# The front of a chunked SSD scan moved into the projection stage of a one-core decoder layer

## The chip, the core and the metric

The kernel runs on one core of one Trainium2 chip. The metric is the device time of one execution in microseconds. The core has TensorE (PE in the profile), VectorE (DVE), ScalarE (ACT), GpSimd (POOL) and SyncE (SP), which issues nearly all of the DMA transfers, in its own order. Each engine runs its instructions in order, and an instruction that waits holds up everything behind it on that engine.

## The reference

One layer of a hybrid decoder for 1024 prompt tokens and 8 samples of 8 new tokens, all in float32. The change touches the Mamba-2 (SSD) branch, which the reference computes in chunks of 128 tokens:

```python
def layer(x, ...):
    x = x + 0.5 * swiglu(rmsnorm(x, norm_ffn1), ffn1_w_in, ffn1_w_out)
    x = x + token_mixing(rmsnorm(x, norm_mix), ...)
    x = x + 0.5 * swiglu(rmsnorm(x, norm_ffn2), ffn2_w_in, ffn2_w_out)

# token_mixing
proj = hn @ w_in                          # u, z, xbc, dt, two gates
branch_pool = pool_mix(u_ext, ...) @ pool_w_out
xbc_c, new_conv = causal_conv(xbc, ...)   # depthwise, width 4, then SiLU
xs, bm, cm = split(xbc_c)                 # 32 heads of 64; 4 groups of B and C, 128 states
dt = softplus(dt_raw + dt_bias)
y, new_ssm = ssd_scan(xs, dt, A, bm, cm, h0)
yg = rms_per_group((y + d_skip * xs) * silu(z))
merged = gate0 * branch_pool + gate1 * ((yg * ssd_norm) @ ssd_w_out)
return merged @ w_o

# ssd_scan, per chunk of 128 tokens
a_cs = cumsum(dt * A);  xdt = x * dt
decay = exp(where(causal, a_cs[l] - a_cs[s], -inf))
cb = einsum('bclgn,bcsgn->bcgls', C, B)
y_diag = einsum('bcgrls,bcsgrp->bclgrp', cb[:, :, :, None] * decay, xdt)
st = einsum('bclgn,bclgr,bclgrp->bcgrpn', B, exp(a_cs[-1] - a_cs), xdt)
h = h * exp(a_cs[-1]) + st                # carried from chunk to chunk
y_off = einsum('bclgn,bcgrpn,bclgr->bclgrp', C, h_prev, exp(a_cs))
```

## The kernel before

The work goes through four stages: the first FFN, the projection (`in_proj`), the mixing stage (`mix`) and the second FFN. Activations lie turned, channels on the partitions and tokens along the row, in two halves `h`: 512 prompt tokens, then 512 prompt tokens and the 64 sample tokens (576). Float32 products are made of three fp32r products (high by high, high by low, low by high); `split` makes the high part on ACT and the low part on DVE, and `load_w` and `wino_weights` do the same with each piece of weight.

The order is written by hand with generators. Dense products run on PE and advance a clock `pe[0]` of nominal PE time; after each few products `tick()` takes every side chain that is due one step further, and a chain says with `yield` how much PE time it lets pass until its next step. `STEP`, `POST`, `RIPE`, `GP` and `MP` are such paces. `tc.high_priority` moves the splitting of weights and the emptying of accumulators ahead of other rows.

In the projection stage `proj_pair` computes two tiles of 128 channels for both halves at once; `done` hands each finished tile to `post_conv` (x, B and C), `post_u`, `post_z` or `post_gate`, whose generators stand in the list `work` and are run one after the other by `worker`. `post_conv` makes the convolution with three DVE instructions (L939), applies SiLU on ACT (L945) and writes the tile to DRAM (`convd`). Tiles of this stage come from a ring `fx` of 17 buffers, and small PSUM tiles from a ring `ps` of 2 banks.

In the mixing stage the dense work is the pool branch (`pgm`, `pbp`), the SSD output product (`pso`) and the output projection (`pwo`). Beside it one chain, `scan`, goes through 8 groups (two halves by four groups of heads), 4 chunks each and one chunk of samples (`smp`) in the second half. Per chunk `ssd_a` loads the cumulated decays spread over all partitions (`ab`), turns x on PE (`pxT`, L167), forms C B on PE and turns B on PE (both in `pcb`), masks C B on DVE (`cbm`, L1312), copies the turned B on ACT (`btok`, L1316), scales the turned x twice on DVE (`xdt`, L1318; `xd`, L1327), and makes the decays on ACT (`ea`, L1335; `ab`, L1337 and L1338) and multiplies them by the masked C B on DVE (L1339). `ssd_st` makes the chunk's state (`pst`, L163) and `ssd_b` the outputs (`pyo`, `pyd`). `gating` and `rstd` follow each group (`pss` sums squares on PE), then `ssd_out` and `merge` use the result. `fetch` loads a group's B, C (`bc`) and x (`xs`) one group ahead. The ring `act` of 42 buffers is shared by all stages; the mixing stage's own tiles lie where the projection's `fx` tiles were.

Of the kernel before, what the change touches and what calls it, by code (L numbers as in the profile page):

```python
# [43 lines left out]
STEP = (5.0, 3.8)  # L44
STEP_S = 1.0
POST, RIPE = 1.0, 3.0
GP = (1.5, 1.2)
# [14 lines left out]
def tile_hybrid_pool_ssd_macaron(  # L62
# [189 lines left out]
    acs_d = [dp.tile([4, NH, CH], F32, tag=f"acsd{h}", name=f"acsd{h}") for h in HALVES]  # L252
# [7 lines left out]
    convd, zd, gd, dhd, dld = (spill(*a) for a in (("cv", 24), ("zd", 16), ("gd", 16), ("dh", KD), ("dl", KD)))  # L260
    xnd = [dp.tile([P, NTOK[0]], F32, tag=f"xn{k}", name=f"xnd{k}") for k in range(KD)]
# [107 lines left out]
    def rstd(tiles, h, count, out, pace=1.0):  # L369
# [13 lines left out]
        yield 2.0 * max(pace, 0.75)  # L383
# [443 lines left out]
    def mix_dt(h, xs):  # L827
# [9 lines left out]
        def chain():  # L837
# [13 lines left out]
            e, s, q, dA = t1[:, 160 : 160 + n], t1[:, 320 : 320 + n], t2[:, :n], t2[:, 160 : 160 + n]  # L851
            dt, acs, dtd, cd = all_[:, :n], all_[:, 160 : 160 + n], all_[:, 320:448], all_[:, 448:576]
# [28 lines left out]
            dma(acs_d[h].rearrange("c h l -> (c h) l"), afm)  # L881
            V.tensor_tensor(dtd, dtd, dt[:, :128], op=ALU.mult)
# [19 lines left out]

    uhist = cp.tile([P, KD, HIST], F32, tag="uhist", name="uhist")
# [6 lines left out]
    def post(gen):  # L910
        work.append((pe[0] + RIPE, gen))
# [12 lines left out]
    def post_conv(h, ct, raw, new):  # L924
# [21 lines left out]
        dma(convd[h][ct], t[:, :N])  # L946
        yield POST / 2
# [112 lines left out]
    def proj_pair(kind, ia, ib, xs):  # L1060
# [4 lines left out]
        while len(work) > 4:  # L1065
            poster[0].step()
# [16 lines left out]
        def after(p, i, bk):  # L1083
# [3 lines left out]
            if p == "1":  # L1087
                out[i] = {"a": fx(name="ra"), "b": fx(name="rb")}
# [161 lines left out]
    def spread(Bf, xs4):  # L1250

        out = []
        for i in range(2):
            tok = slice(512 + 32 * i, 544 + 32 * i)
            xr = act((P, 5, 96), name="xr")
            S.copy(xr[:, :4, :].rearrange("p j (r t) -> p j r t", r=3), xs4[:, :, tok].unsqueeze(2).broadcast_to([P, 4, 3, 32]))
            S.copy(xr[:, 4, :].rearrange("p (r t) -> p r t", r=3), Bf[:, tok].unsqueeze(1).broadcast_to([P, 3, 32]))
            out.append(xr)
        return out
# [20 lines left out]
    def ssd_a(h, g, c, Bf, Cf, xs4, dts, h0s):  # L1280
# [11 lines left out]
        for q in range(nq):  # L1292
            ab = act((P, hq, L), name="ab")
            if smp:
                dma(ab, acs_sd[g * HPG : (g + 1) * HPG].partition_broadcast(P))
            else:
                r0 = g * HPG + q * hq
                dma(ab, acs_d[h][c, r0 : r0 + hq].partition_broadcast(P))
            abs_.append(ab)
        if smp:  # L1300
            xrs = spread(Bf, xs4)
            h0s.update({i: load_state(g, u) for i, u in enumerate(UNITS[:3])})
        yield
# [7 lines left out]
        cbm = small((P, P), "cbm", 2)  # L1311
        V.tensor_tensor(cbm[:L, :L], pb[:L, :L], tri_s if smp else tri, op=ALU.mult)  # L1312
        btok = None
        if not smp:
            btok = small((P, P), "btok", 2)
            S.copy(btok, pb[:, 128:256])  # L1316
        xp = act((P, 512), name="xdt")
        V.tensor_tensor(xp[:L, :].rearrange("p (h d) -> p h d", d=HD), px[:L, :].rearrange("p (h d) -> p h d", d=HD),  # L1318
                        dt[:L, hcs].unsqueeze(2).broadcast_to([L, HPG, HD]), op=ALU.mult)
        if smp:  # L1320
            xd = []
# [3 lines left out]
        else:  # L1325
            xd = act((P, 512), name="xd")
            V.tensor_tensor(xd[:L, :].rearrange("p (h d) -> p h d", d=HD), px[:L, :].rearrange("p (h d) -> p h d", d=HD),  # L1327
                            dtd[:L, hcs].unsqueeze(2).broadcast_to([L, HPG, HD]), op=ALU.mult)
        G.tensor_tensor(xs4[:, :, tok], xs4[:, :, tok], Dcol[:, g * 4 : g * 4 + 4].unsqueeze(2).broadcast_to([P, 4, L]), op=ALU.mult)
        ea = act((P, 4, L), name="ea")  # L1330
        for q, ab in enumerate(abs_):
            av = ab.rearrange("p (q h) l -> p q h l", h=2)
            ev = ea[:, q * (hq // 2) : (q + 1) * (hq // 2), :]
            for hh in range(2):
                S.activation(ev[hh * HD : (hh + 1) * HD], av[hh * HD : (hh + 1) * HD, :, hh, :], AF.Exp)  # L1335
            for i in range(hq):
                S.activation(ab[:L, i, :], ab[:L, i, :], AF.Relu, bias=acs[:L, hc + q * hq + i : hc + q * hq + i + 1], scale=-1.0)  # L1337
            S.activation(ab[:L], ab[:L], AF.Exp, scale=-1.0)  # L1338
            V.tensor_tensor(ab[:L], ab[:L], cbm[:L, :L].unsqueeze(1).broadcast_to([L, hq, L]), op=ALU.mult)  # L1339
# [10 lines left out]
    def ssd_b(h, g, c, a, hold, Cf, y4, dts, h0s):  # L1350
# [8 lines left out]
        if smp:  # L1359
# [12 lines left out]
            for i, (pr, bh) in enumerate(units):  # L1372
# [12 lines left out]
                dma(dst, h0)  # L1385
                if pr == 3:
# [19 lines left out]
        for i in range(HPG):  # L1406
            m_ = abs_[i // abs_[0].shape[1]][:L, i % abs_[0].shape[1], :]
# [32 lines left out]
    def ssd_group(h, g, Bf, Cf, xs4, dts, zs):  # L1440
# [3 lines left out]
        for c in range(4 + h):  # L1444
            ga = ssd_a(h, g, c, Bf, Cf, xs4, dts, h0s)
            next(ga)
            if c == 3:
# [310 lines left out]
```

## Time and profile before

| what | value |
| --- | --- |
| median of 3 runs | 2921.1 us (2917.12 to 2922.39) |
| the profiled execution | 2922.54 us |
| its span | 2920.7 us, 52612 instructions |
| mean granted TensorE clock | 0.99 |
| PE busy | 2829.0 us, 97% |
| DVE, ACT, POOL busy | 1715.2, 1374.7, 1001.9 us |
| HBM read, written | 361.77 MB, 143.05 MB |

Time is read on PE, which is busy 97% of the span: what counts is what fills it and where it stands still. The mixing stage runs from 1505 to 2166 us of the span, the projection from 803 to 1505 us.

### The profile page before, as it was taken

The page shows a single profiled execution, that of the slowest core. Times are in us where ns is not written, and L with a number is a line of the kernel's source. Part 1 is how long each engine was busy: PE and PEld are TensorE (multiplying, and loading weights), DVE is VectorE, ACT ScalarE, POOL GpSimd, SP SyncE. Part 2 cuts the span into 40 slices and gives each one's busy share as a digit, 9 for nine tenths or more (in the row PEclk, how much of TensorE's full clock was granted, in tenths as well). Part 3 has the DMA queues.
Part 4 walks back from the last instruction along what each step waited for, and adds up shares of the span by engine and source line. Part 5 has one row for each costly group of instructions (what it writes and reads, how often), then busy time and mean ns, then how long its engine had stood idle before and what let it go on. Part 6 is the DMA issues. An engine that isn't in the chain of part 4 may idle for free.

```text
span 2920.7 us, 52612 instructions
## 1 busy us (share of the span) xinstructions
PE 2829.0 (97%) x19306; PEld 2612.3 (89%) x19306; DVE 1715.2 (59%) x2722; ACT 1374.7 (47%) x3024; POOL 1001.9 (34%) x1088
## 2 busy tenths in 40 slices
PE   7999999999999999999989999889999999999998
PEld 6999999789989999999977887678999999997898
DVE  6555555434383586766767777866665544453432
ACT  5444444323354555554556665576233444442322
POOL 6444444000132355464712332322134444440000
PEclk9999999999999999999999999999999999999999
DMA  4575454856445554633377777785774522236642
GB/s 136 165 226 183 159 170 132 284 184 192 120 128 164 162 191 155 201 111 124 107 232 247 242 229 227 242 265 176 247 233 146 165 92 82 78 109 209 217 155 73
DMA packets 530340, 508.09 MB, mean 174 GB/s; under 512 B 36885, under 2 KB 374665, under 8 KB 530073
## 3 DMA queue, kind: packets, MB, share of 16 engines
q1 hardware_dynamic: 530064, 504.72, 54.6%
q8 instruction: 152, 2.49, 0.4%
q14 instruction: 108, 0.88, 0.1%
q10 hardware_dynamic: 16, 0.00, 0.0%
HBM read 361.77 MB, written 143.05 MB: 173 GB/s over the span
## 4 chain that ended last, share of the span: by engine, by line
PE 47%; DVE 4%; DMA 3%; ACT 2%; issue 1%; SPq 1%; POOL 0%; POOLq 0%; ACTq 0%; DVEq 0%
PE pw L163 24%; PE po L163 9%; PE pso L163 4%; PE pbp L163 3%; PE pwo L163 2%; PE pg L163 1%; PE pu L163 1%; ACT ab L1337 1%; PE pyd L163 1%; PE pst L163 1%; DVE ab L1339 1%; DMA ab<-acsd 0%; PE pyo L163 0%; DVE xs L1484 0%; DMA wh<-part 0%
## 5 line engine op out<-in xcount | busy, mean ns | idle before, releaser
L163 PE MATMUL pw<-X,wh 128*128 128x288 f32 (+2 forms) x2832 | 626.9, 310 | 4.7 <-ACT v L560 3.6
L163 PEld LDWEIGHTS pw<-X,wh 128*128 128x128 f32 x2832 | 461.7, 189 | 27.3 <-ACT v L560 4.5
L163 PE MATMUL pw<-X,wl 128*128 128x288 f32 (+1 forms) x1644 | 473.5, 288 | 0.7 <-DVE wl L444 0.7
L163 PE MATMUL pw<-hl,wh 128*128 128x256 f32 (+1 forms) x1536 | 392.1, 328 | 0.9 <-DVE t L564 0.9
L444 DVE TENSOR_TENSOR wl<-s,wh 128x512 fp32r<-128x512 f32 x288 | 227.2, 789 | 239.8 <-ACT wh L443 214.1
L163 PE MATMUL pw<-hi,wh 128*128 128x288 f32 x1120 | 331.1, 296 | 1.0 <-ACT t L596 1.0
L163 PE MATMUL pw<-hi,wl 128*128 128x288 f32 x1120 | 329.8, 294 | 0.0
L163 PE MATMUL pw<-lo,wh 128*128 128x288 f32 x1120 | 329.7, 294 | 0.0
L437 POOL TENSOR_TENSOR s<-wraw,wraw 128x512 f32<-128x512 f32 x144 | 195.7, 1359 | 358.2 <-DVE wl L444 259.3
L295 DVE TENSOR_TENSOR wl<-wraw,wh 128x512 fp32r<-128x512 f32 x228 | 163.7, 719 | 253.2 <-ACT wh L294 240.3
L163 PEld LDWEIGHTS pw<-X,wl 128*128 128x128 f32 x1644 | 311.6, 190 | 0.9 <-DVE wl L444 0.9
L163 PE MATMUL pw<-hl,wl 128*128 128x256 f32 x1072 | 300.3, 280 | 0.0
L294 ACT ACTIVATE wh<-wraw 128x512 fp32r<-128x512 f32 x228 | 137.8, 606 | 328.7 <-PE po L163 228.1
L163 PEld LDWEIGHTS pw<-hl,wh 128*128 128x128 f32 x1536 | 259.0, 189 | 21.8 <-DVE t L564 1.1
L443 ACT ACTIVATE wh<-s 128x512 fp32r<-128x512 f32 x288 | 181.1, 630 | 163.2 <-PE pw L163 138.8
L444 DVE TENSOR_TENSOR wl<-wraw,wh 128x512 fp32r<-128x512 f32 x216 | 168.9, 782 | 137.6 <-ACT wh L443 131.0
L163 PEld LDWEIGHTS pw<-hi,wh 128*128 128x128 f32 x1120 | 210.5, 188 | 7.9 <-ACT t L596 1.8
L163 PE MATMUL po<-hh,wh 128*128 128x288 f32 (+1 forms) x800 | 211.0, 324 | 4.0 <-ACT hh L355 3.5
L163 PE MATMUL po<-hr,wh 128*128 128x288 f32 (+1 forms) x800 | 210.9, 323 | 0.0
L163 PE MATMUL po<-hh,wl 128*128 128x288 f32 (+1 forms) x800 | 210.7, 322 | 0.1
L163 PEld LDWEIGHTS pw<-lo,wh 128*128 128x128 f32 x1120 | 210.6, 188 | 0.0
L163 PEld LDWEIGHTS pw<-hi,wl 128*128 128x128 f32 x1120 | 210.1, 188 | 0.0
(374 smaller groups left out, 6259.2 us busy)
## 6 DMA issues: line engine op xcount, KB each, us to landing
wraw<-in_ffn_w_in_dram SPq DMA_DIRECT2D x188, 256.0 KB
wh<-part SPq DMA_DIRECT2D x156, 256.0 KB
wl<-part SPq DMA_DIRECT2D x156, 256.0 KB
wraw<-in_w_in_dram SPq DMA_DIRECT2D x144, 256.0 KB
wraw<-in_ffn_w_out_dram SPq DMA_DIRECT2D x120, 256.0 KB
part<-ph SPq DMA_DIRECT2D x80, 256.0 KB
part<-pr SPq DMA_DIRECT2D x80, 256.0 KB
ab<-acsd SPq DMA_DIRECT2D x64, 256.0 KB
```

Of the source, the lines that this page charges most:

```text
L163: T.matmul(out, lhsT, rhs, start=start, stop=stop, skip_group_check=free)
L294: S.activation(wh, raw, AF.Copy)
L295: V.tensor_tensor(wl, raw, wh.bitcast(F32), op=ALU.subtract)
L437: G.tensor_tensor(t, a, b, op=op)
L443: S.activation(wh, a, AF.Copy)
L444: V.tensor_tensor(wl, a, wh.bitcast(F32), op=ALU.subtract)
L1337: S.activation(ab[:L, i, :], ab[:L, i, :], AF.Relu, bias=acs[:L, hc + q * hq + i : hc + q * hq + i + 1], scale=-1.0)
L1339: V.tensor_tensor(ab[:L], ab[:L], cbm[:L, :L].unsqueeze(1).broadcast_to([L, hq, L]), op=ALU.mult)
```

## The change

The front of the scan is made in the projection stage for the four chunks of a half at a time, written to DRAM and loaded by the scan:

- `tokens`, posted by `post_conv` for each x tile: 4 turns on PE, one multiplication by dt on DVE (128 by 512), a write to `xpd`. `pairs`, posted when B and C of a group are there: 4 turns of B, a copy on ACT and a write to `btd`; 4 products C B, one masking multiplication on DVE (128 by 512) and a write to `cbd`.
- In the scan a chunk loads `xdt` from `xpd`, 256 KB; `cb` and `bt` are loaded per group by `fetch` in place of B (of B only the 64 sample columns are loaded, `bs`). `xd` is now made from `xdt` in SBUF. The sample chunks keep their own front.
- The decays in DRAM stand in the order even heads, odd heads, so that `ea` takes two ACT instructions of 64 by 512 per chunk where it took four of 64 by 256.
- Paces: `STEP` 5.0, 3.8 to 4.7, 3.4; `POST` 1.0 to 0.7; `proj_pair` lets 7 rather than 4 posts wait; `gating` waits 2.5 longer ahead of `pss` (`G_WAIT`). For the second half z is loaded later, after sample unit 4.
- The last pair of gates takes its tiles from the ring `act`, and the scan takes its first step, its first loads, ahead of the pool branch (`cs.step()`).
- In `merge` of the first half the product is added to the accumulator first, then multiplied by the gate on DVE, then the pool branch is added on POOL; its loads are issued two tiles ahead.

```diff
-STEP = (5.0, 3.8)
-STEP_S = 1.0
-POST, RIPE = 1.0, 3.0
-GP = (1.5, 1.2)
+STEP = (4.7, 3.4)
+STEP_S, Z_UNIT = 1.0, 4
+POST, RIPE, RIPE_2 = 0.7, 3.0, 2.5
+GP, G_WAIT = (1.5, 1.2), 2.5
...
-        yield 2.0 * max(pace, 0.75)
+        yield wait + 2.0 * max(pace, 0.75)
...
-            dma(acs_d[h].rearrange("c h l -> (c h) l"), afm)
-            V.tensor_tensor(dtd, dtd, dt[:, :128], op=ALU.mult)
+            for i in range(HPG):
+                dma(acs_d[h][:, :, i % 2, i // 2, :].rearrange("c g l -> (c g) l"), afm[i::HPG])
...
         dma(convd[h][ct], t[:, :N])
+        if ct < 16:
+            post(tokens(h, ct, t), RIPE_2)
+        else:
+            ready[h, ct] = t
+            if ct >= 20:
+                post(pairs(h, ct - 20, ready.pop((h, ct - 4)), ready.pop((h, ct))), RIPE_2)
+        yield POST / 2
+
+    def tokens(h, ct, t):
+
+        g, j = ct // 4, ct % 4
+        pt = psum("ps", "pxT")
+        for c in range(4):
+            tr(pt[:, c * CH : (c + 1) * CH], t[:, c * CH : (c + 1) * CH], ident)
+        yield POST
+        o = fx(name="xp")[:, :512]
+        k = g * HPG + 2 * j
+        V.tensor_tensor(o.rearrange("p (c e d) -> p c e d", e=2, d=HD), pt.rearrange("p (c e d) -> p c e d", e=2, d=HD),
+                        dtl[h][:, :, k : k + 2].unsqueeze(3).broadcast_to([P, 4, 2, HD]), op=ALU.mult)
+        dma(xpd[h][g].rearrange("(c t) n -> t c n", t=CH)[:, :, j * P : (j + 1) * P], o.rearrange("p (c n) -> p c n", n=P))
+        yield POST / 2
+
+    def pairs(h, g, Bt, Ct):
+
+        pt = psum("ps", "pbT")
+        for c in range(4):
+            tr(pt[:, c * CH : (c + 1) * CH], Bt[:, c * CH : (c + 1) * CH], ident)
+        yield POST
+        o = fx(name="bt")[:, :512]
+        S.copy(o, pt)
+        dma(btd[h][g], o)
+        pt = psum("ps", "pcb")
+        for c in range(4):
+            tok = slice(c * CH, (c + 1) * CH)
+            mm(pt[:, tok], Bt[:, tok], Ct[:, tok])
+        yield POST
+        o = fx(name="cb")[:, :512]
+        V.tensor_tensor(o.rearrange("p (c l) -> p c l", l=CH), pt.rearrange("p (c l) -> p c l", l=CH),
+                        tri.unsqueeze(1).broadcast_to([P, 4, CH]), op=ALU.mult)
+        dma(cbd[h][g], o)
         yield POST / 2
...
-        while len(work) > 4:
+        while len(work) > 7:
...
-                out[i] = {"a": fx(name="ra"), "b": fx(name="rb")}
+                new = act if len(xs) == 1 else fx
+                out[i] = {"a": new(name="ra"), "b": new(name="rb")}
...
+            xp = act((P, 512), name="xdt")
+            dma(xp, xpd[h][g][tok, :])
         yield
-        px = psum("ps", "pxT")
-        for j in range(4):
-            tr(px[:L, j * P : (j + 1) * P], xs4[:, j, tok], ident)
-        pb = psum("ps", "pcb")
-        mm(pb[:L, 0:L], Bf[:, tok], Cf[:, tok])
-        if not smp:
-            tr(pb[:L, 128:256], Bf[:, tok], ident)
...
+            cbm, btok = cb[:, tok], bt[:, tok]
             xd = act((P, 512), name="xd")
-            V.tensor_tensor(xd[:L, :].rearrange("p (h d) -> p h d", d=HD), px[:L, :].rearrange("p (h d) -> p h d", d=HD),
-                            dtd[:L, hcs].unsqueeze(2).broadcast_to([L, HPG, HD]), op=ALU.mult)
+            V.tensor_tensor(xd.rearrange("p (h d) -> p h d", d=HD), xp.rearrange("p (h d) -> p h d", d=HD),
+                            dtd[:, hcs].unsqueeze(2).broadcast_to([P, HPG, HD]), op=ALU.mult)
...
-            if c == 3:
-                for j in range(4):
...
+            if c == 3 and h == 0:
+                load_z(h, g, zs)
...
-        Bf, Cf = (small((P, 576), "bc", 4)[:, :N] for _ in range(2))
+        Cf, cb, bt = (small((P, 576), "bc", 6)[:, :n] for n in (N, 512, 512))
...
     cs = start(scan())
+    cs.step()
...
+                    if h == 0:
+                        V.tensor_tensor(acc[m][:, a:b], acc[m][:, a:b], pt[:, : b - a], op=ALU.add)
...
+            if h == 0:
+                V.scalar_tensor_tensor(t1[m], t1[m], 1.0, acc[m], op0=ALU.add, op1=ALU.mult)
+                G.tensor_tensor(t1[m], t1[m], acs[m], op=ALU.add)
```

The order of instructions moves at three places. The first is PE in the mixing stage, inside the SSD output product (`pso`), where the second chunk of the fourth group's scan is worked in. Before:

```order
L163 MATMUL pso_20767<-yhl_19469,wl_20770 128x512
L163 MATMUL pst_20775<-xd_20675,btok_20671 128x512
L167 MATMUL pxT_20780<-ident,xs_3549_19806 128x128 x4
L163 MATMUL pcb_20785<-bc_19805,bc_19804 128x128
L167 MATMUL pcb_20785<-ident,bc_19804 128x128
L163 MATMUL pso_20767<-yhl_19507,wh_20768 128x512 x2
```

Of the change, at the same chunk (`bc` is now the turned B that `fetch` loaded):

```order
L163 MATMUL pso_21017<-yhl_19966,wh_21018 128x512 x2
L163 MATMUL pso_21017<-yhl_19966,wl_21020 128x512
L163 MATMUL pst_21028<-xd_20923,bc_20151 128x512
L163 MATMUL pso_21017<-yhl_19990,wh_21018 128x512 x2
L163 MATMUL pso_21017<-yhl_19990,wl_21020 128x512
```

The four turns, the product C B and the turn of B are gone from behind `pst`; the dense product goes on at once.

The second is DVE in the projection stage, where the second tile of the first group's first pair of x tiles is convolved. Before (`wl` splits weights, `ct` is the convolution, `ra` and `rb` empty PE's accumulators, `pr` splits weights of a later stage):

```order
L444 TENSOR_TENSOR wl_11902<-s_2150_11899,wh_11901 128x512
L939 SCALAR_TENSOR_TENSOR ct_11826<-rb_11378,cols,ct_11826 128x512
L444 TENSOR_TENSOR wl_11952<-wraw_11697,wh_11951 128x512
L1112 TENSOR_TENSOR rb_11717<-pw_2117_11703,rb_11717 128x256
L939 SCALAR_TENSOR_TENSOR ct_11920<-rb_11398,cols,ct_11920 128x512 x2
L1112 TENSOR_TENSOR rb_11737<-pw_2121_11723,rb_11737 128x288
L444 TENSOR_TENSOR wl_12030<-wraw_12021,wh_12029 128x512
```

Of the change (`cb` is the masked C B, `xp` the scaled x of `tokens`):

```order
L447 TENSOR_TENSOR wl_12182<-s_2198_12179,wh_12181 128x512
L944 SCALAR_TENSOR_TENSOR ct_12010<-rb_11420,cols,ct_12010 128x512
L989 TENSOR_TENSOR cb_12055<-pcb_12050,tri 128x512
L944 SCALAR_TENSOR_TENSOR ct_12010<-rb_11420,cols,ct_12010 128x512 x2
L989 TENSOR_TENSOR cb_12071<-pcb_12066,tri 128x512
L969 TENSOR_TENSOR xp_12079<-pxT_12074,dt_9032 128x512
L969 TENSOR_TENSOR xp_12087<-pxT_12082,dt_9546 128x512
L447 TENSOR_TENSOR wl_12237<-s_2197_12177,wh_12236 128x512
```

Between two splits of weights there are now seven instructions of the posts, four of them new, and each of the four waits for PE's turns or products.

The third is SP where the mixing stage begins. Before (`gd` is the write of the last gates, `dts`, `bc` and `xs` are the scan's first loads, `d` a load of the pool branch):

```order
L916 DMA gd_5_221<-rb_18385 128x576
L1298 DMA ab_18555<-acsd_115 128x512
L1298 DMA ab_18557<-acsd_115 128x512
L291 DMA wraw_18855<-in_pool_w_out_dram 128x4x128
L1506 DMA dts_18535<-dtp_272 128x576
L1498 DMA bc_18537<-cv_16_136 128x512
L1499 DMA bc_18538<-cv_20_140 128x512
L1501 DMA xs_3248_18539<-cv_0_120 128x512
```

Of the change:

```order
L294 DMA wraw_19115<-in_pool_w_out_dram 128x4x128
L1559 DMA dts_18938<-dtp_296 128x576
L1546 DMA bc_18942<-btd_0_280 128x512
L1547 DMA bc_18941<-cbd_0_272 128x512
L1548 DMA bc_18940<-cv_20_140 128x512
L1554 DMA xs_3339_18943<-cv_0_120 128x512
L1554 DMA xs_3339_18943<-cv_1_121 128x512
L921 DMA gd_4_220<-ra_18802 128x576
L1554 DMA xs_3339_18943<-cv_2_122 128x512
L921 DMA gd_5_221<-rb_18803 128x576
```

The scan's first loads have moved ahead of the writes of the last gates; they are more by one `bc` for each of two groups and by one `xdt`. The pool branch's load `d` of its last group stands 13 rows behind `dts` before and 24 rows behind it now.

More of the change, by code (lines that the diff above doesn't have):

```diff
@@ L367, in along, with rstd @@
         tr(out, r[:n, i : i + 1].broadcast_to([n, P]), ident[:n, :n])
-    def rstd(tiles, h, count, out, pace=1.0):
+    def rstd(tiles, h, count, out, pace=1.0, wait=0.0):
         N = NTOK[h]
@@ L1348, in load_state, with ssd_b @@
         return t
-    def ssd_b(h, g, c, a, hold, Cf, y4, dts, h0s):
+    def ssd_b(h, g, c, a, hold, Cf, y4, dts, h0s, zs):
         dt, acs, dtd, cd, cdp = dts
@@ L1438, in ssd_st, with load_z, ssd_group @@
         return hold
-    def ssd_group(h, g, Bf, Cf, xs4, dts, zs):
+    def load_z(h, g, zs):
+        for j in range(4):
+            z = act((P, NTOK[h]), name="z")
+            dma(z, zd[h][g * 4 + j])
+            zs.append(z)
+    def ssd_group(h, g, Bs, Cf, cb, bt, xs4, dts, zs):
         y4 = xs4
@@ L1477, in gating @@
         rr = []
-        yield from rstd([y4[:, j, :N] for j in range(4)], h, 512, rr, GP[0])
+        yield from rstd([y4[:, j, :N] for j in range(4)], h, 512, rr, GP[0], G_WAIT)
         while h * NG + g - 2 >= freed[0]:
@@ L1566, in merge, with load @@
         merged = [0]
+        acs = [None] * KD
+        def load(m):
+            if h == 0 and m < KD:
+                t1[m], acs[m] = act((P, N), name="t1"), act((P, N), name="ac")
+                dma(t1[m], gd[h][KD + m])
+                dma(acs[m], accd[h][m])
         def head():
@@ L1576, in head @@
                 merged[0] += 1
-        ch = start(head(), MP)
+        if h == 1:
+            ch = start(head(), MP)
+        for m in range(2):
+            load(m)
         yn = ynorm(h, gs)
@@ L1581, in merge @@
         for m in range(KD):
+            load(m + 2)
             pb = dense(ssd_w_out[0], gs[0] * 4, 4 * len(gs), m * P, [yn], name="pso")[0]
-            while merged[0] <= m:
+            while h == 1 and merged[0] <= m:
                 ch.step()
```

92 lines of the change are left out of this document (52 added, 40 removed).

## The prediction

> **What bounds the kernel now.** I read the page's list of engines first, then a table of stages, then PE's waits in the mixing stage.
>
> ```profile
> PE 2829.0 (97%) x19306; PEld 2612.3 (89%) x19306; DVE 1715.2 (59%) x2722; ACT 1374.7 (47%) x3024; POOL 1001.9 (34%) x1088
> ```
>
> PE sets the time. The table of stages has per stretch its length and the busy time of PE, PEld, DVE, ACT and POOL, then the granted clock, the DMA share and GB/s. The second row is the projection, the next five the mixing stage.
>
> ```profile
> 803.00:1505.00 702.00, 698.22 (x5418) 688.83 (x5416) 483.86 (x766) 375.21 (x788) 335.43 (x459) 1.00 0.48 153
> 1505.00:1525.00 20.00, 11.10 (x44) 8.00 (x44) 8.63 (x13) 12.39 (x27) 1.04 (x1) 0.81 0.92 320
> 1525.00:1730.00 205.00, 200.17 (x1330) 171.39 (x1330) 148.08 (x239) 131.34 (x323) 62.55 (x49) 0.99 0.75 234
> 1730.00:1890.00 160.00, 145.19 (x903) 110.83 (x902) 125.61 (x181) 98.61 (x266) 54.56 (x44) 0.96 0.75 238
> 1890.00:2010.00 120.00, 106.60 (x742) 86.48 (x743) 79.36 (x120) 76.69 (x212) 43.35 (x34) 0.93 0.72 221
> 2010.00:2166.00 156.00, 153.73 (x1194) 148.44 (x1194) 98.16 (x154) 54.59 (x122) 31.87 (x26) 1.00 0.75 243
> ```
>
> The projection leaves PE idle for 702.0 - 698.2 = 3.8 us; the mixing stage's rows add to 661.0 us with 616.8 us of PE, 44.2 us idle, and a clock of 0.81 to 0.96 where the idle time lies. So PE work that the change carries from one stage to the other weighs the same in both, and a gain can only come from these 44 us and the clock they cost. Who ends the idle time (total us, times, longest), in the mixing stage:
>
> ```profile
> PE pss L163 <- DVE ssq L380: 6.6, 3, 2.7
> PE pgm L163 <- DMA d<-dh: 4.4, 1, 4.4
> PE pst L163 <- ACT ab L1337: 4.3, 1, 4.3
> PE pxT L167 <- DMA xs<-cv: 3.9, 4, 3.0
> PE pyd L163 <- ACT btok L1316: 2.7, 2, 1.7
> PE pwo L163 <- DVE t L1588: 2.6, 1, 2.6
> PE pst L163 <- DVE xd L1327: 1.7, 2, 1.3
> PE pb L167 <- DVE cbm L1312: 1.1, 1, 1.1
> ```
>
> The edit touches most of these rows directly: `pxT`, `btok`, `xd` and `cbm` belong to the moved front.
>
> **The change part by part.** PE's own work first. One front as the timeline has it (start, length), between two dense products, and one block of four turns inside dense products of an earlier stage:
>
> ```profile
> 1572.53 0.60 PE L167 MATMUL pxT<-ident,xs 128*128 128x128 f32 x4
> 1572.97 0.39 PE L163 MATMUL pcb<-bc,bc 128*128 128x128 f32 x2
> 1573.22 0.48 PE L163 MATMUL pbp<-fh,wh 128*128 128x512 f32 x1
> ...
> 185.16 0.60 PE L167 MATMUL ptr<-ident,xin 128*128 128x128 f32 x4
> 185.51 0.38 PE L163 MATMUL pw<-hi,wh 128*128 128x288 f32 x1
> ```
>
> A front holds PE from 1572.53 to 1573.22, 0.69 us; 32 of them leave the mixing stage, -22 us. The projection gets 32 blocks of x and 8 of B, 40 by 0.35 = 14 us, and 32 products C B by 0.25 us (1573.22 - 1572.97, the turn of B included, so a high figure), 8 us: +22 us. I take 0 for the sum, with -2 to +4 if each block breaks into a dense run at a small cost.
>
> **The start of the mixing stage.** The pieces of the chain of waits, start and length, there:
>
> ```profile
> 1506.53 4.42 DMA gd<-rb
> ...
> 1511.02 0.32 SPq L1506
> ...
> 1511.87 0.42 SPq L1499
> ...
> 1512.33 0.43 SPq L1501
> ...
> 1513.29 5.65 DMA xs<-cv
> ...
> 1519.00 5.36 DMA d<-dh
> ...
> 1524.50 4.64 PE pgm L163 x12
> ```
>
> The scan's first load waits until the write of the last gates has left the memory that it will use; then x, and behind x in SP's order the pool branch's last operands `d`. PE waits 3.9 us for x at `pxT` and 4.4 us for `d`, 8.3 us, at a clock of 0.81. With the last gates in the other ring nothing holds the first load, and no PE row waits for x. But `d` now stands 24 rows behind `dts` instead of 13: 11 more issues at 0.46 us (SP's rows from 1511.87 to 1512.33 are one) are 5 us, against a start that is earlier by the write's 4.42 us and by the time until the gates are there, some 10 us as I judge it. I take -7 us; the ends are -10 (all idle time and the lost clock) and 0 (`d` as late as now).
>
> The clock of 0.81 in these 20 us has its low in a finer cut:
>
> ```profile
> 1520.00:1530.00 10.00, 5.63 (x18) 4.21 (x18) 4.47 (x7) 7.80 (x19) 1.04 (x1) 0.61 0.91 284
> ```
>
> The Trainium skill, "TensorE: Matmul & The Clock Gate", section "What's actually happening", says that the clock falls to half after an idle window of about 3.4 us and comes back after about as long of work; the trace agrees: the row of 0.61 holds the wait of 4.4 us. By that rule the wait costs 1.7 us beyond itself; by the row of 0.81 it is up to 3.8 us, idle time included, and the sum goes by the row.
>
> **Waits for the front elsewhere.** `btok` 2.7, `xd` 1.7 and `cbm` 1.1 make 5.5 us. These sources are gone or no longer wait for PE. What may be late next is the decay chain on ACT and DVE, which the shorter `STEP` also brings on sooner, so I count -4, ends -5.5 and 0.
>
> **DVE, ACT and POOL in the scan.** Groups of the mixing stage, count, busy us and mean ns:
>
> ```profile
> L1318 DVE TENSOR_TENSOR xdt<-pxT,dts 128x512 f32<-128x512 f32 x32 | 21.8, 681 | 0.6 <-PE pxT L167 0.3
> L1327 DVE TENSOR_TENSOR xd<-pxT,dts 128x512 f32<-128x512 f32 x32 | 21.7, 678 | 0.0
> L1339 DVE TENSOR_TENSOR ab<-ab,cbm 128x512 f32<-128x512 f32 x64 | 55.0, 861 | 30.1 <-ACT ab L1338 30.1
> L1312 DVE TENSOR_TENSOR cbm<-pcb,tri 128x128 f32<-128x128 f32 x32 | 9.0, 282 | 11.2 <-PE pcb L167 11.2
> L1335 ACT ACTIVATE ea<-ab 64x256 f32<-64x256 f32 x136 | 55.9, 411 | 18.9 <-DMA ab<-acsd 17.3
> L1316 ACT COPY btok<-pcb 128x128 f32<-128x128 f32 x32 | 8.4, 263 | 58.9 <-DVE cbm L1312 55.1 <-DMA xs<-cv 3.7
> L1338 ACT ACTIVATE ab<-ab 128x512 f32<-128x512 f32 x64 | 39.5, 618 | 0.1
> ```
>
> DVE loses 21.8 + 9.0 = 31 us; `xd` stays, but reads SBUF as L1339 does, and may rise from 678 to 861 ns, 6 us back. ACT loses 8.4 us of `btok`, and 128 instructions of 411 ns (53 us) become 64 of 512 columns at L1338's 618 ns (40 us): -21 us. This frees no PE time by itself. But between 1730 and 1890 DVE is busy 125.6 of 160 us while PE idles 15, and 1890 to 2010 PE idles 13. I count 4 us of PE's idle time there and 2 us of clock: -6, ends -12 and 0.
>
> **Gating and merge.** `G_WAIT` puts 2.5 us of other PE work ahead of `pss`, whose three waits are 6.6 us, the longest 2.7: -5, ends -6 and 0. In `merge` of the first half a DVE addition per tile goes from the tail; POOL's takes its place, and the rows that could get longer are the waits of `pwo` for the last tiles (2.6 us now): -2, ends -4 and +3.
>
> **What is added.** The scan reads 32 `xdt` of 256 KB and 2 instead of 1 tile per group in place of B, some 10 MB. Beside it the DMA share is 0.72 to 0.75. SP issues `xdt` behind `ab`, so `ab` waits for nothing new; `xdt` lands an issue later. I take +3 us for chunks where a load comes late, ends 0 and +10: the whole of `ab`'s waits on ACT today is 17.3 us, in the row of L1335. `xpd` is written in runs of 512 B. So is the state of the samples read, and a load of it takes no longer than one of 2304-byte rows (the chain of waits, start and length):
>
> ```profile
> 1785.76 5.56 DMA h<-in_state_ssm_dram
> 1610.61 5.63 DMA z<-zd
> ```
>
> "DMA: Bandwidth & Descriptors", section "Specifications", of the Trainium skill puts the least piece for full rate at 512 B; the row agrees. The sample decays `ab` now come in pieces of 256 B, below it, four loads a step ahead of their use; no run here shows their price. At nothing I put the 14 further small writes of decays at the projection's start, whose cover is the whole projection, and the later load of z in the second half, which has the rest of the sample units to land in against 5.63 us; without that cover each of the four groups would wait those 5.63 us once, on DVE.
>
> **The projection.** DVE gets 40 instructions of 128 by 512 out of PSUM at 0.68 us, 27 us on 483.9 of 702, ACT 8 copies. These join the convolutions, where DVE is fullest (two stretches of 16 us):
>
> ```profile
> 1056.00:1072.00 16.00, 16.00 (x130) 16.00 (x129) 15.60 (x26) 9.07 (x20) 11.70 (x16) 1.00 0.64 209
> 1200.00:1216.00 16.00, 15.29 (x121) 15.07 (x120) 15.90 (x27) 6.95 (x16) 4.63 (x3) 1.00 0.53 179
> ```
>
> In the second of them DVE is busy 15.9 of 16 us and PE loses 0.7 us. Queued behind a new `xp` that waits for PE's turns stand the splits of weights, for which PE waits in turn. What hides it is the lead of these splits, which `high_priority` moves ahead. I take +5 us, ends 0 and +27 (all added DVE time exposed).
>
> The sum: 0 - 7 - 4 - 6 - 5 - 2 + 3 + 5 = -16 us. The profiled execution took 2922.5 us, 1.4 us over the median of the runs; so 2921.1 - 16 = 2905 us.
>
> **The rivals.** *The projection pays.* DVE is where the change decides: if its queue in the convolution stretches grows longer than the lead of the weight splits, about one product of a pair, each added instruction there holds PE. For it speaks 15.9 of 16 us; against it 3.8 us of PE idle in the whole stage now, and the 7 posts that may wait for emptier stretches. At the full +27 instead of +5 the sum is +6: 2927 us. *DMA pays.* The 10 MB at 284 GB/s (the row at 1520) are 35 us of transfer; if a third of that falls where the share is above 0.9 and weights are waited for, it is +12 instead of +3, and the 4 + 6 us gained in the scan go too: +3, 2924 us. Against it: no weight load in the mixing stage is among PE's longer waits. *Nothing moves.* The front's waits pass to the next producer, `ab`, whose own wait is already 4.3 us: only the start and gating stay, with both prices: -7 - 5 + 3 + 5 = -4, 2917 us. *More goes.* The ends of the gains add to 10 + 5.5 + 12 + 6 + 4 = 37.5 us; four fifths of them without a price are -30, 2891 us, and if the clock of the row of 0.93 comes back whole over its 120 us, 8 us more: 2883. By the Trainium skill's clock rule (the page and section above) that follows once no wait is over 3.4 us.
>
> **How the numbers follow.** Forecast 0.50 (2892 to 2914 in itself), more 0.12, nothing moves 0.14, the projection pays 0.17, DMA pays 0.07. About 0.2%, 5.8 us, is what a measurement of this kernel can tell from no change: faster 0.62, same 0.14, slower 0.24. The range reaches from 2882, the far side of "more", to 2931, past the price of a full projection; less than 2 in 10 is left out.
>
> **What would show it.** Right: PE's idle time in the mixing stage at 20 to 30 us, no row of PE waiting for `xs` or `btok`, `pss` under 2 us, the first gap under 4 us, the projection stage longer by 22 to 30 us. Wrong: PE in the projection waiting for `wl` or for its accumulators to be emptied, by more than 15 us; new waits of PE or DVE for `xdt`; or the wait of `pst` as long as now.

## The result: slower by 1.06%

| kernel | median | runs |
| --- | --- | --- |
| before | 2921.55 us | 2917.12 to 2922.39, 4 runs |
| after | 2952.39 us | 2947.71 to 2953.53, 4 runs |

The ratio is 1.0106, with a 95% interval of 1.0088 to 1.0123. The prediction was 2905 us, with a range of 2882 to 2931.

The engines' busy times in the page of the kernel after:

```profile
PE 2844.4 (96%) x19306; PEld 2621.4 (89%) x19306; DVE 1699.3 (58%) x2692; ACT 1364.0 (46%) x2940; POOL 999.6 (34%) x1088
```

PE has the same 19306 matmuls. The table of stages of the kernel after: the projection, the first 20 us of the mixing stage, the whole mixing stage.

```profile
805.00:1543.00 738.00, 726.94 (x5648) 714.80 (x5647) 506.43 (x805) 383.91 (x798) 330.04 (x460) 1.00 0.52 163
1543.00:1563.00 20.00, 11.48 (x40) 7.65 (x40) 8.68 (x12) 11.42 (x23) 8.51 (x8) 0.83 1.06 351
1543.00:2191.00 648.00, 597.88 (x3962) 502.37 (x3962) 417.11 (x632) 352.83 (x847) 198.64 (x153) 0.96 0.80 257
```

The mixing stage of the kernel before, in the same form:

```profile
1505.50:2161.00 655.50, 611.79 (x4185) 521.06 (x4186) 457.59 (x700) 371.44 (x939) 193.38 (x153) 0.97 0.75 238
```

PE idles 11.1 us in the projection (3.8 before) and 50.1 us in the mixing stage (43.7 before). The stage that was to gain has more idle time, though DVE and ACT have less to do there. Its first 20 us are as empty as before. PE's waits in the mixing stage of the kernel after:

```profile
PE pst L163 <- DVE xd L1371: 19.7, 8, 4.7
PE pst L163 <- issue: 6.1, 1, 6.1
PE pgm L163 <- DVE fl L362: 3.3, 3, 1.9
...
PE pyd L163 <- DVE ab L1382: 1.6, 1, 1.6
...
PE pss L163 <- DVE ssq L383: 0.5, 2, 0.3
```

and DVE's own:

```profile
DVE xd L1371 <- DMA xdt<-xpd: 25.8, 14, 3.9
...
DVE xd L1371 <- DMA ab<-acsd: 5.5, 1, 5.5
```

The rows of `btok` and of `xs` at `pxT` are gone, `pss` is at 0.5 us. In their place stands one row of 19.7 us: PE waits at the state product for `xd`, and DVE, which makes `xd` out of the loaded `xdt`, waits 25.8 us for that load. One place, the first chunk of the group that starts near 1826 us; SP's rows and then DVE's:

```profile
1826.33 0.39 SPq L1516 DMA_DIRECT2D out_dram<-fin  x1
1826.76 0.98 SPq L1344 DMA_DIRECT2D ab<-acsd  x2
1827.78 0.45 SPq L1351 DMA_DIRECT2D xdt<-xpd  x1
```

```profile
1833.67 1.27 DVE L1371 TENSOR_TENSOR xd<-xdt,dts 128x512 f32<-128x512 f32 x1 [3.66 <-DMA xdt<-xpd]
```

The load stands in SP's queue behind the store of the state before it (`fin`) and two loads of `ab`, goes out at 1827.8, and DVE can start 5.9 us later, having waited 3.66 us.

The load is not behind the whole of the 19.7 us. Ahead of four of the eight waits DVE sat idle for `xdt`, and these four make 11.3 us of PE's time. Ahead of the other four, 8.4 us, DVE came straight from other work, as here, ahead of the longest one (PE goes on at 1850.06, after 4.7 us):

```profile
1846.71 1.75 DVE L362 SCALAR_TENSOR_TENSOR ml<-t,mh 128x512 fp32r<-128x512 f32 x1
1848.38 0.67 DVE L1655 TENSOR_TENSOR acc<-acc,pso 128x512 f32<-128x512 f32 x1
1848.98 0.93 DVE L1371 TENSOR_TENSOR xd<-xdt,dts 128x512 f32<-128x512 f32 x1
```

PE's waits in the projection of the kernel after:

```profile
PE pcb L163 <- ACT so L1089: 4.2, 4, 2.0
PE pg L163 <- DVE wl L298: 2.1, 3, 1.2
PE pxT L167 <- DVE xp L969: 1.7, 2, 0.8
PE pxT L167 <- ACT so L1089: 1.7, 2, 1.2
```

The new turns wait 7.6 us for accumulators that ACT and DVE have yet to empty.

**A measure for all the runs.** Idle time doesn't hold what PE loses at the lower clock. So for each stage I add up, from the records of PE's matmuls, the time from each start to the next, and take off what that form costs when nothing waits (230 ns for 512 columns, 132 for 288, 120 for 256, and so on, the same for every kernel). The rest is called *beyond*; only its differences are read. The projection is counted from the first turn of dt (`pdtT`) to the first `pgm`, the mixing stage from there to the first `pg`. "Ratio" is to the kernel before, in runs on the same chip. The kernel before had medians of 2918.4 to 2921.6 us beside the different runs, so a difference of medians can be some 3 us off: by the ratios e1 is 15.5 us faster than the kernel after where the medians say 16.6, e3 8 and not 9, e4 26 and not 28.

| kernel | median, us | ratio | projection, beyond | mixing, beyond |
| --- | --- | --- | --- | --- |
| before | 2921.6 | 1 | 699.3, 10.3 | 655.2, 53.2 |
| after | 2952.4 | 1.0106 | 733.3, 20.3 | 647.7, 70.2 |
| e1 xdt a chunk earlier | 2935.8 | 1.0053 | 733.4, 20.5 | 631.7, 54.2 |
| e2 scan's old paces | 2936.1 | 1.0052 | 734.6, 21.7 | 636.9, 59.4 |
| e3 projection's old paces | 2943.3 | 1.0080 | 730.2, 17.3 | 644.5, 67.0 |
| e4 x in the scan | 2924.5 | 1.0017 | 714.5, 15.5 | 640.1, 48.6 |
| e5 e4, all old paces | 2916.7 | 0.9988 | 712.3, 13.3 | 637.0, 45.5 |
| e6 before + `G_WAIT` | 2927.7 | 1.0022 | 699.3, 10.3 | 659.5, 57.6 |
| e7 before + start | 2915.0 | 0.9976 | 699.3, 10.3 | 646.3, 44.4 |
| e8 before + merge | 2918.2 | 0.9991 | 699.3, 10.3 | 654.3, 52.4 |
| e9 after, chunk 0 first | 2950.5 | 1.0110 | 734.1, 21.2 | 647.8, 70.3 |
| e10 after, all mended | 2934.6 | 1.0059 | 730.5, 17.5 | 634.0, 56.5 |
| e11 before + start + merge | 2914.3 | 0.9981 | 699.3, 10.4 | 647.3, 45.4 |
| e12 x in the scan, mended | 2908.3 | 0.9959 | 711.4, 12.4 | 628.4, 37.0 |
| e13 e12 + 32 loads | 2920.9 | 1.0004 | 712.0, 13.0 | 633.8, 42.3 |
| e14 e12 + 32 small loads | 2914.6 | 0.9980 | 712.2, 13.2 | 632.8, 41.3 |
| e15 x moved, 2nd half | 2934.4 | 1.0049 | 744.5, 38.5 | 620.8, 36.4 |
| e16 e11, chunk 0 first | 2906.6 | 0.9956 | 698.6, 9.6 | 641.2, 39.3 |
| e17 e15, new paces | 2916.2 | 0.9983 | 722.7, 16.7 | 624.1, 39.6 |
| e18 x moved, 1st half | 2945.6 | 1.0091 | 728.9, 22.9 | 649.5, 65.0 |

Before to after: the projection is 34.0 us longer, of which 10.0 beyond and so 24.0 of matmuls; the mixing stage is 7.5 us shorter, with 24.4 us fewer of matmuls and 17.0 more beyond. Together that is 26.5 of the 30.1 us by which the span grew; 2.9 lie ahead of the projection, where profiles of these kernels differ by up to 3 us anyway, and 0.7 behind the mixing stage.

### The profile page after: what moved, and what is told of

Same layout as the page of the kernel before. It is cut to its first block, busy times and chain, and to the rows that moved or that the text cites. A ratio compares the mean times of both kernels' runs of the same rounds, so it can differ in the third digit from the quotient of the medians.

```text
span 2950.8 us, 52769 instructions
## 1 busy us (share of the span) xinstructions
PE 2844.4 (96%) x19306; PEld 2621.4 (89%) x19306; DVE 1699.3 (58%) x2692; ACT 1364.0 (46%) x2940; POOL 999.6 (34%) x1088
## 4 chain that ended last, share of the span: by engine, by line
PE 83%; DMA 6%; DVE 4%; ACT 3%; POOL 2%; issue 2%; SPq 1%; POOLq 0%; ACTq 0%; DVEq 0%
PE pw L163 44%; PE po L163 17%; PE pso L163 5%; PE pg L163 3%; PE pwo L163 2%; PE pbp L163 2%; PE pu L163 2%; DMA xdt<-xpd 1%; PE pst L163 1%; PE pyd L163 1%; PE pyo L163 1%; PE pgm L163 1%; DMA hr<-hd 1%; DMA ab<-acsd 1%; DMA wraw<-in_ffn_w_in_dram 1%
## 5 line engine op out<-in xcount | busy, mean ns | idle before, releaser
L447 DVE TENSOR_TENSOR wl<-s,wh 128x512 fp32r<-128x512 f32 x288 | 219.5, 763 | 246.9 <-ACT wh L446 222.9
L297 ACT ACTIVATE wh<-wraw 128x512 fp32r<-128x512 f32 x228 | 137.9, 607 | 333.0 <-PE po L163 220.2
L446 ACT ACTIVATE wh<-wraw 128x512 fp32r<-128x512 f32 x216 | 135.7, 628 | 164.5 <-PE pw L163 139.9
```

Of the source, the lines that this page charges most:

```text
L297: S.activation(wh, raw, AF.Copy)
L446: S.activation(wh, a, AF.Copy)
L447: V.tensor_tensor(wl, a, wh.bitcast(F32), op=ALU.subtract)
```

## The experiments

**Is the load of x late?** The theory: `xd` now hangs on a load that lands too late. e1 loads each `xdt` one chunk earlier (code is shown shortened, here and below).

```diff
-            xp = act((P, 512), name="xdt")
-            dma(xp, xpd[h][g][tok, :])
+            xp = xpre.pop(0)          # loaded during the chunk before
+            load_x(h, g, c + 1)       # at chunk 3: chunk 0 of the next group
```

> The changed kernel with each load of xdt issued one chunk earlier (chunk c+1's while chunk c begins; chunk 0's while chunk 3 of the group before begins). Late-load theory: PE's waits for xd (19.7 us after the change, 8 times) fall under 5 us and DVE's waits for the xdt loads (25.8 us) under 8 us; the time falls from 2952 by 15 to 22 us, to 2930 to 2937. Rival, DVE's queue: xd comes late because DVE is busy with the merge and with ab, so PE's waits for xd stay above 12 us and the time stays within 5 us of 2952.

e2 and e3 put back paces, e4 the x part of the front (with its load and `tokens` gone):

```diff
-STEP = (4.7, 3.4)
+STEP = (5.0, 3.8)                             # e2
-POST, RIPE, RIPE_2 = 0.7, 3.0, 2.5
+POST, RIPE, RIPE_2 = 1.0, 3.0, 3.0            # e3
-        while len(work) > 7:
+        while len(work) > 4:                  # e3
+            for j in range(4):                # e4, in ssd_a
+                tr(px[:, j * P : (j + 1) * P], xs4[:, j, tok], ident)
```

> The changed kernel with the scan's paces of before, STEP (5.0, 3.8) for (4.7, 3.4). Late-load theory: a chunk has three such steps between the load and the state product, so the load gains 0.9 to 1.2 us of cover; PE's waits for xd fall from 19.7 us to 12 to 16 us and the time by 2 to 8 us, to 2944 to 2950. Rival, compressed scan: the shorter paces are the cause, PE's waits for xd fall under 6 us and the time to 2928 to 2936.

> The changed kernel with the projection's paces of before (POST 1.0 for 0.7, ripe 3.0 for the new steps, at most 4 waiting steps for 7). Theory that the projection's 10 us beyond its matmuls come from the tighter paces (PE waits for the so copies and xp, 7.6 us): PE's waits there fall under 3 us, the time falls by 4 to 8 us, to 2944 to 2948. Rival, that they come from the added steps themselves (two more PSUM tiles to be emptied per column tile): the waits stay or rise and the time is 2950 to 2960. The late-load theory has the waits for xd in the mixing stage unchanged in both.

> The changed kernel with the x part made in the scan again (4 turns and the product with dt per chunk; no tokens step, no xdt written or loaded); B's turns and the masked C B stay in the projection. PE has the same matmuls. Late-load theory: PE's waits for xd fall under 5 us, waits for xs and the turns return with 2 to 5 us, the projection is shorter by 11 us of turns and 3 to 5 us of waits, the mixing stage longer by 11 us of turns less 15 to 20 us of waits: 2928 to 2936. Rival, that the pace of the scan and the merge are the cause: PE's idle time in the mixing stage stays as it is and the time is 2945 to 2952.

Measured: 2935.8 (interval of the ratio 1.0038 to 1.0068), 2936.1 (1.0035 to 1.0069), 2943.3 (1.0059 to 1.0101) and 2924.5 (1.0008 to 1.0027). PE's waits of e1:

```profile
PE pst L163 <- DVE xd L1383: 5.7, 5, 2.8
PE pst L163 <- issue: 4.3, 1, 4.3
```

The wait for `xd` falls from 19.7 to 5.7 us and the time by 16.6: the lateness is shown. DVE's row for `xdt`, 25.8 us, is gone (4.6 us at the start, put down to `ab`, stay), and 5.7 us lies within what PE waits for `xd` in kernels that load no `xdt` (0.8 in e4; 5.8 in e16 and 6.4 in e12, below). In e4, where no load stands behind `xd`, its row of PE's waits is down to 0.8 us and the time falls by 28 us, more than was expected. e2 answers to neither theory: `xd` still holds PE for 15.7 us, as the late load has it, yet the time fell as in e1 and almost as the compressed scan has it, so the shorter steps cost something besides (ahead of its two longest waits, 14.2 us together, DVE idled for the load for 4.8 us only). In e3 the new turns' waits for accumulators went, the waits of `pw` rose from 0.4 to 3.8 us, and 9 us were won, more than the projection shows (3.1 us); another 3.2 us are in the mixing stage, which e3 doesn't edit.

**What do the edits beside the front do?** e5 is e4 with the paces of e2 and e3. e6, e7 and e8 put one part of the change each into the kernel before:

```diff
+        yield wait + 2.0 * max(pace, 0.75)    # e6: G_WAIT = 2.5 ahead of pss
+                new = act if len(xs) == 1 else fx   # e7
+    cs.step()                                  # e7
```

e8 takes over `merge` as it stands in the change.

> As e4 (x part in the scan, pairs kept in the projection), with the paces of before in the scan and the projection (STEP 5.0 and 3.8, POST 1.0, at most 4 waiting steps). Late-load theory: without the xdt load the scan's pace has little left to cure, so STEP gives 0 to 3 us; the projection's paces give the 3 us of PE waits for so copies: 2918 to 2924. Rival, that the paces by themselves cost (as much as e2's 16 us and e3's 9 us): 2905 to 2912.

> The kernel before with the gating's wait of 2.5 us ahead of the row sums and nothing else. As the prediction has it: PE's waits for ssq (6.6 us) fall under 2 us and the time by 3 to 6 us, to 2913 to 2916. Rival, that PE only waits elsewhere for the same chain: 2917 to 2920, with the waits moved to t, ab or yhl.

> The kernel before with the gate tiles out of the act ring and the scan's first step taken at its start, and nothing else. As the prediction has it: the first gap of the mixing stage (7.9 us) falls by 5 to 8 us, time 2911 to 2914. Rival, that the first loads land at the rate of a full DMA and ACT then waits for ab ahead of the weight copies: the gap keeps 5 to 8 us under another name and the time is 2917 to 2920.

> The kernel before with the changed merge alone. Prediction: 0 to 4 us faster, 2914 to 2919. Rival, that the three products after the last group put DVE and POOL on the path ahead of the output projection: 2 to 6 us slower, 2921 to 2925, with PE waiting for mh or for POOL's t.

e5 is at 2916.7 (ratio 0.9979 to 0.9997), between its two expectations. e6 is slower than either of its own, 2927.7 (1.0013 to 1.0032): PE's waits for the gating and for what stands behind it, first before, then e6:

```profile
PE pss L163 <- DVE ssq L380: 6.6, 3, 2.7
...
PE pwo L163 <- DVE ml L359: 0.9, 1, 0.9
```

```profile
PE pbp L163 <- DVE fl L359: 3.5, 1, 3.5
PE pss L163 <- DVE ssq L380: 3.4, 2, 1.8
...
PE pwo L163 <- DVE ml L359: 2.7, 2, 2.4
...
PE pwo L163 <- ACT mh L355: 2.3, 2, 2.0
```

3.2 us are won at `pss` and 7.6 us come back at `fl`, `ml` and `mh`. That the later gating pushes these copies back on ACT and DVE is how I read it; no run tests it. e7 is faster, 2915.0 (0.9967 to 0.9986), as the prediction had it for the start; e8 is at 2918.2 (0.9982 to 1.0001), within its 0 to 4 us but hardly told from no change.

**Can the move pay once nothing is late?** In e9 the loads of a group's chunk 0 go out ahead of the seven loads of the next group. e10 has this, e1, the old paces and no `G_WAIT`; e11 is e7 with e8; e12 is e5 with this order and no `G_WAIT`.

```diff
-            nxt = fetch(*todo[i + 1]) if i + 1 < len(todo) else None
-            yield from ssd_group(h, g, *cur, dts[h], zs)
+            gen = ssd_group(h, g, *cur, dts[h], zs)
+            step = next(gen)                  # chunk 0's loads
+            nxt = fetch(*todo[i + 1]) if i + 1 < len(todo) else None
+            yield step
+            yield from gen
```

> The changed kernel with the loads of a group's chunk 0 (ab and xdt) issued ahead of the next group's seven loads instead of behind them, and nothing else. Theory that the late xdt is a place in SP's queue: at the start the 6.1 us wait for the first state product falls to 1 to 3 us, the waits of 3 to 4 us at the first state products of groups 5 to 7 (3.0, 3.8 and 3.6 us) go, and the time is 2936 to 2943. Rival, that all loads are late since the DMA is full: these waits stay over 3 us each and the time is 2948 to 2953.

> The changed kernel with all that the runs so far name mended: xdt loaded one chunk earlier, chunk 0's loads ahead of the next group's, paces of before in scan and projection, no wait in the gating. Theory that the move itself gains what the prediction named once nothing is late: 2905 to 2912 (e1 gave 17 us, e3 9, the waits overlap; the start 4). Rival, that the front's move gains nothing net, since the projection pays 10 us of waits for what the scan is relieved of: 2917 to 2925.

> The kernel before with the start's two edits (e7) and the new merge (e8). If the two add: 2921 less 6 less 3, so 2911 to 2913. If the merge's 3 us are chance: 2914 to 2916.

> e5 (x part in the scan, pairs in the projection, paces of before) without the wait in the gating and with chunk 0's loads ahead of the next group's. The gating's wait cost 6 us alone in the kernel before: if it does so here too, 2908 to 2912; if it only hid behind other waits here, 2915 to 2918.

e9 gains nothing (1.0095 to 1.0125): the start's wait falls to 2.7 us as expected, the others at `pst` only from 19.7 to 14.2. PE's waits from the projection on, and ACT's in the mixing stage up to 1760 us:

```profile
PE pst L163 <- DVE xd L1371: 14.2, 8, 3.6
...
PE pbp L163 <- DVE wl L298: 4.9, 1, 4.9
PE pbp L163 <- ACT wh L297: 3.8, 2, 2.7
...
PE pst L163 <- issue: 2.7, 1, 2.7
```

```profile
ACT wh L297 <- DMA wraw<-in_pool_w_out_dram: 14.5, 5, 8.7
```

What `pst` gains, 9 us, `pbp` loses: the pool branch's weights are late now, 14.5 us of ACT's waits against 0.3 us in the kernel after. The late load has only changed its name. e10 (1.0042 to 1.0075) came out above both of its expectations. PE's wait for the pool branch's weights, and ACT's up to 1760 us:

```profile
PE pbp L163 <- ACT wh L297: 6.6, 2, 4.9
```

```profile
ACT wh L297 <- DMA wraw<-in_pool_w_out_dram: 17.0, 9, 5.5
```

The time is e1's. e11 is at 2914.3 (0.9972 to 0.9991), no faster than e7, so the merge adds nothing to the start. e12 is at 2908.3 (0.9944 to 0.9973): faster than both kernels, with x back in the scan. Where the DMA stood some 60 us into the mixing stage, before and then after (columns as above, DMA share next to last):

```profile
1565.00:1605.00 40.00, 38.37 (x238) 31.05 (x236) 32.45 (x50) 26.31 (x66) 12.87 (x9) 1.00 0.69 223
```

```profile
1603.00:1643.00 40.00, 37.36 (x223) 30.50 (x222) 27.34 (x43) 25.47 (x59) 8.98 (x7) 0.96 0.97 298
```

**Bytes, queue, or place?** e13 adds a load of 256 KB per chunk, which nothing reads, to e12; e14 the same with one row of 2 KB. e15 moves x for the second half of the tokens alone, e18 for the first alone, both else as e10. e17 is e15 with the changed kernel's paces in the projection. e16 is e11 with chunk 0's loads first. (e13 and e14 also give `cb` and `bt` a ring of their own, with as many buffers as before.)

```diff
+            dma(small((P, 512), "extra", 1), convd[h][4 * g + c][:, :512])   # e13
+            dma(small((P, 512), "extra", 1)[:1], convd[h][4 * g + c][:1, :512])   # e14
+            if h == 1:                        # e15 and e17; h == 0 in e18
+                post(tokens(h, ct, t), RIPE_2)
```

> e12 (2908) with one more load of 256 KB per chunk, 32 in all, at the place in SP's queue where the changed kernel loads xdt, into a tile that nothing reads. Traffic or queue theory: other loads land later (weights of the pool's second product, ab), 2916 to 2930. Theory that only the wait for xdt itself costs: 2906 to 2911.

> e13 with one row of 2 KB in place of 256 KB per load: the same issues and the same queue, hardly any bytes. Traffic theory: 2906 to 2911. Queue theory (SP's 0.65 us per issue delays what stands behind): as e13, 2916 to 2930.

> e10 with x made in the projection and loaded for the second half of the tokens alone (16 loads of 256 KB), and turned in the scan for the first half. Traffic theory: the first 150 us of the mixing stage, where the DMA is fullest, are as in e12, and the second half pays little: 2909 to 2918. If the loads cost wherever they stand: halfway between e12 and e10, 2919 to 2924, or above.

> e11 (before, with the start's edits and the new merge, 2914) with chunk 0's loads ahead of the next group's. If the pairs made in the projection gain nothing, this reaches e12's 2906 to 2911; if they gain 4 to 8 us, it stays at 2912 to 2917.

> e15 with the changed kernel's paces in the projection (POST 0.7, ripe 2.5 for the new steps, at most 7 waiting steps). If e15's waits for so copies came of the steps' crowding at 4: the projection falls from 744.5 us to 722 to 730 and the time to 2912 to 2920; the mixing stage stays at 621. If they are the price of the added steps: the time stays within 5 us of 2934.

> The mirror of e15: x made in the projection and loaded for the first half alone, turned in the scan for the second. Theory that the loads cost where DMA and SP are fullest, in the first 150 us: PE's time beyond its matmuls in the mixing stage is 48 to 58 us, as in e10 (56.5), against 36 to 37 in e15 and e12. Rival, that it is spread: 40 to 46 us.

Against e12's ratio of 0.9959 (0.9944 to 0.9973), e13's 1.0004 (0.9993 to 1.0014) is 13 us more and e14's 0.9980 (0.9971 to 0.9990) 6 us, give or take some 5, between its two theories: by these the issues alone cost about half and the bytes the rest. The split is not shown: the profiled executions of the two are only 1.3 us apart, with 5.3 and 4.3 us more beyond in the mixing stage than e12. e15 missed its time but its mixing stage is beyond by 36.4 us, e12's figure; what it lost stands in the projection, PE's waits there:

```profile
PE pxT L167 <- ACT so L1090: 9.0, 2, 5.4
PE puh L167 <- ACT so L1090: 4.4, 4, 2.2
```

e17 (2916.2, 0.9974 to 0.9993) takes that away with the paces alone, 744.5 to 722.7 us. Why e10, with more steps at the same paces, escapes it is open. e18 is the mirror and has the loss: 65.0 us beyond in the mixing stage, above the 48 to 58 expected. ACT's waits up to 1760 us in e18, then in e17:

```profile
ACT wh L297 <- DMA wraw<-in_pool_w_out_dram: 17.5, 9, 5.6
```

```profile
ACT wh L297 <- DMA wraw<-in_pool_w_out_dram: 8.6, 2, 6.5
```

So the loads of x cost in the first half, where the pool branch's weights come over the same queue and DMA; in the second half, loaded a chunk ahead, they cost next to nothing in the mixing stage. The place is plain: over the first 250 of the stage's 2448 dense products, some 75 to 95 us, PE is 17 us further beyond in e10 than in e16 and 19 us in e18 than in e12, and over the whole stage 17 and 28.

How the loads cost that much there is not shown. In e13, where the same 32 loads go out a chunk later and nothing reads them, ACT's row for the pool branch's weights is 17.9 us, as long as in e10. Yet e13 is only 6 us further beyond than e12 in those first 250 products, and PE's row for these weights is short:

```profile
PE pbp L163 <- ACT wh L297: 1.3, 1, 1.3
```

So the late weights are part of it, ACT's row is not their price, and the rest is open.

e16 is at 2906.6 (0.9939 to 0.9972), the fastest here, and at e12's time: the pairs made in the projection gain nothing, 2.8 us more beyond there and 2.3 less in the mixing stage.

e10 and e16 differ in the front (with `xdt`'s lead and the later load of z in the second half): 1.0059 against 0.9956, 30 us. The slowdown is thus the front's, some 17 us beyond more in the mixing stage and 8 in the projection. By e12 it is that of x and not of the pairs. What came with it, start (-6 us), merge (0 to -3) and `G_WAIT` (+6), about cancels.

## Why the prediction was wrong

- **The added loads**, +3 us with ends 0 and +10, is the term that failed. The bound was taken from `ab`'s waits on ACT, off PE's path, but DVE stands still at `xd` until the load lands, and PE waits behind it: 25.8 us on DVE, and on PE 11.3 of the row of 19.7 and the 6.1 at the start. By moving the load alone e1 gets back 16.6 us, and leaving x in the scan (e4) 28. The text named "new waits of PE or DVE for xdt" as what would show it wrong; they are the largest row.
- **The rival "DMA pays"** came nearest. Its price of 12 us for the traffic is about that of the 32 loads without a reader (e13, 13 us); what it left out is the wait for the loads themselves. The objection to it, that no weight load was among PE's longer waits, held for the traffic of before: with the loads of x mended, PE waits 6.6 us for the pool's weights (e10).
- **The start**, -7 us: right by itself (e7: -6.3 us), gone in the change. PE waited 8.3 us there for x and `d`, and waits 6.1 + 1.9 + 0.6 = 8.6 us now: `pst` for `xdt` (the row "issue"), `fl` and `d`. DVE's 5.5 us ahead of that first `xd` are put down to `ab` in the profile, but `xd` reads `xdt` and `dts` alone; that it is `xdt` is read from the code. The step asked what is late next for `d` and not for the `xdt` that the same change puts behind two groups' loads.
- **Waits for the front elsewhere**, -4 us: `btok` and the rows for x are gone as foretold, and the wait of `pst` for `xd`, 1.7 us, is 19.7 us.
- **DVE, ACT and POOL in the scan**, -6 us: the front's own rows fell as counted (`xd` takes 856 ns in the mean against the 861 estimated; half of them take under 0.7 us, as before, and a few up to 1.7), and DVE by more than that, from 457.6 us busy in the mixing stage to 417.1. PE got nothing for it that these runs show: e12, with the pairs moved, and e16 are equal, and moving x of the second half as well leaves the stage at 36.4 and 39.6 us beyond (e15, e17) against e12's 37.0. Its end of 0 was the right value.
- **Gating**, -5 us: the sign was wrong. `pss` fell to 0.5 us, under the 2 us foretold, and the wait alone costs 6.4 us (e6).
- **Merge**, -2 us: -3 (e8), hardly told from no change, and nothing on top of the start (e11 beside e7); within its ends.
- **PE's matmuls**, 0 with -22 and +22: +24.0 and -24.4, right.
- **The projection**, +5 us with ends 0 and +27: 10.0 us beyond. The waits are at the accumulators of the new turns, not at the weight splits that were feared; the rival of a full price did not come.

PE's waits in the first 25 us of the mixing stage of the kernel after:

```profile
PE pst L163 <- issue: 6.1, 1, 6.1
PE pgm L163 <- DVE fl L362: 1.9, 1, 1.9
PE pgm L163 <- DMA d<-dh: 0.6, 1, 0.6
```

The groups that carry DVE's figures, in the mixing stage and in the projection of the kernel after:

```profile
L1371 DVE TENSOR_TENSOR xd<-xdt,dts 128x512 f32<-128x512 f32 x32 | 27.4, 856 | 31.3 <-DMA xdt<-xpd 25.8 <-DMA ab<-acsd 5.5
L969 DVE TENSOR_TENSOR xp<-pxT,dt 128x512 f32<-128x512 f32 x32 | 21.4, 682 | 4.4 <-PE pxT L167 4.0
```

By stage: the terms forecast +27 us for the projection and -43 for the mixing stage; measured are +34.0 and -7.5. Of the 47 us between 2905 and 2952, 36 were lost in the mixing stage and 7 in the projection.

## What to carry to other kernels

A result that is made early, stored and loaded again swaps a wait for an engine (1.7 us here) for a wait for a load (19.7 us), which must be given its lead: count the queue places ahead of the load and the bytes that land with it, and look at the stretch where the DMA is fullest, not at the stage's mean. Relief of engines that don't set the time bought nothing here: count it only where a row shows PE waiting for them. Test the small edits that travel with a large one each by itself: here the order of the loads, the start and the merge alone made the faster kernel (e16, 2906.6 us), and the large edit cost 30 us.

## What the runs showed of the hardware

32 loads of 2 KB, for which nothing waits, cost some 6 us, give or take 5 (0.9980 against 0.9959), about 0.2 us each. In the 14 cases of the kernel after in which DVE sat idle for `xdt`, a load of 256 KB, it started 5.0 to 7.2 us after SP's issue, 5.9 in the rows shown. The Trainium skill, "SBUF — State Buffer", section "The DMA setup-cost knee", fits a transfer by 2 us plus its bytes at 436 GB/s, which makes an estimate of 2.6 us for 256 KB; the trace has about twice that and more, the issue and DVE's start included, and the lead of a load goes by the trace.
